# A transformer layer with an expert block: where and in what portions the dense gate table is written to DRAM

## The chip, the cores and the metric

The kernel runs on one core of one Trainium2 chip. The metric is the device time of one execution in microseconds (us), as a median over several runs. The engines named below are TensorE (PE, matmuls; PEld is its weight load), VectorE (DVE), ScalarE (ACT), GpSimd (POOL) and SyncE (SP). SP, ACT and POOL also issue DMAs; a "q" behind the name (ACTq) means the engine's own sequencer, which waits, branches and issues.

## The reference

256 latent tokens pass through one layer: a token mixer, and then a PEER block, which is what matters here. Each token has 8 heads, each head picks 16 of 16384 single-neuron experts, and the block sums the picked experts:

```
idx = e1 * PEER_NKEYS + e2
g = jax.nn.softmax(sc, axis=-1)
u_sel = jnp.take(u_tab, idx, axis=0)
act = jax.nn.gelu(jnp.einsum('td,thkd->thk', hb, u_sel))
v_sel = jnp.take(v_tab, idx, axis=0)
return jnp.einsum('thk,thkd->td', (g * act.astype(jnp.float32)).astype(hb.dtype), v_sel)
```

## The kernel before, in words

The kernel does not gather the experts of each token. It multiplies all 256 tokens by all 16384 rows of `u_tab`, 128 rows at a time, in 128 steps (`u_step`), and writes the GELU of each 128 x 256 result into a table in DRAM, `agd`: one row per expert, and in it, for each half of the tokens (`t`), 128 activations and 128 gates. The gates come from the routing and are dense too, with zeros for experts that a token did not pick. Afterwards a list of the experts in use is made, and only their rows of `v_tab` and of `agd` are gathered, in 92 tiles of 128 rows (`N_L`), and multiplied on TensorE (`v_tile`).

Each float32 operand is split into a high and a low part (ACT at L252, then DVE at L253), and each product is made of three matmuls (`mm3`, L281 to L283). The split of a tile has two halves, one at the start of a step (`ahead2`) and one at k == 7 of the matmul loop (`behind`), and it runs two tiles ahead of the matmuls. The raw u tiles (1 MB each) lie in four slots, `O_RAW`; SP loads a slot again (`done`, `emit_load`, L102) as soon as the split of the tile in it has ended.

The work that has nothing to do with the u products (routing, gates, list) is a Python generator, `beneath`, which `fill` draws on once per `u_step`, behind the step's matmuls, up to a budget. So its instructions are spread over the steps in program order. The generator `gates` makes the gates in batches of 8 tokens: DVE builds one-hot matrices, PE multiplies them (`products`, L1041 and L1044), and ACT copies the result out of PSUM into one of two buffers `GC` (`keep`, L1051). One buffer holds 64 tokens (`HT`, a half tile): 128 x 128 x 64 values, 4 MB. When it is complete, `keep` writes it to `agd` with four DMAs of 1 MB on ACT's queue (L1056). There are four half tiles, so this happens four times. Behind it in ACT's program stand the GELU of the step (L1176) and the store of its 128 KB (L1177), and then the split of the next tile (L252). `places` (its first matmul is L1087) and `make_list` come after the gates.

Behind the last u step the second product begins. Its v rows come with indirect DMAs on POOL (`gather(n)`, 1 MB), the rows of `agd` with others (`act_rows(n)`), both issued by the helper line L894. Gathers 0 to 3 are issued from `beneath`; the later ones come from `emit_load`, each when a slot has become free: 4 to 7 when the u tiles 124 to 127 are split, 8 and 9 when the v tiles 0 and 1 are. DVE makes a tile's weights from the gathered rows (`weights`, L1187; `weights_low`, L1201) with a copy on ACT (L1196) in between. Between `act_rows(1)` and `act_rows(2)` lies a branch, `tc.If(more > 0)` (L1255), for lists that are too long; with these inputs it isn't taken.

Of the kernel before, what the change touches and what calls it, by code (L numbers as in the profile page):

```python
# [29 lines left out]
N_L = N_A + N_1  # L30
# [11 lines left out]
N_RAW, N_HL = 4, 5  # L42
# [8 lines left out]
def layer_kernel(ctx: ExitStack, tc: tile.TileContext, I, out, dbg=None):  # L51
    nc = tc.nc
# [35 lines left out]
    order = []  # L88
    pos = [0]
    loaded = set()  # L90

    def emit_load(i):
        if i < len(order):
            loaded.add(i)
            key, parts = order[i]
            if parts is None:
                if key[1] + N_RAW < N_L:
                    gather(key[1] + N_RAW)
                return
            base = O_RAW + (i % N_RAW) * D  # L100
            for o, n, src in parts:
                nc.sync.dma_start(fa[:, base + o:base + o + n], src)  # L102
# [173 lines left out]
    def behind():  # L276
        if pending:
            pending.pop()()
# [583 lines left out]
    HT = 64  # L862
# [169 lines left out]

    def gates():
        def products(b):
            counts = pb[4 + b // NB][:, 0:P]
            oj, og = pair(b, P)
            for i in range(TB):
                oa = OHA[b % 2][:, i, :]  # L1040
                TE.matmul(counts, oa, oj[:, i, :], start=b % NB == 0 and i == 0,  # L1041
                          stop=b % NB == NB - 1 and i == TB - 1, skip_group_check=True)
                for q in range(2):
                    TE.matmul(pb[6 + i // 4][:, (i % 4) * P:(i % 4 + 1) * P], oa, og[:, i, q, :],  # L1044
                              start=i % 4 == 0 and q == 0, stop=q == 1, skip_group_check=True)

        def keep(b):
            c, o = divmod(b, HT // TB)
            for x in range(2):
                tl = slice(o * TB + 4 * x, o * TB + 4 * x + 4)  # L1050
                S.activation(GC[c % 2][:, :, tl], pb[6 + x].rearrange("p (t j) -> p j t", j=P), AF.Copy,  # L1051
                             scale=1.0 / GSC)
            if o == HT // TB - 1:
                for x in range(4):
                    cs = slice(32 * x, 32 * x + 32)
                    S.dma_start(ag4[cs, :, c // 2, 1, (c % 2) * HT:(c % 2 + 1) * HT].rearrange("c e i -> e c i"),  # L1056
                                GC[c % 2][:, cs, :])

        for b in range(2 * NB + 2):
            sl = slice(b * TB, (b + 1) * TB)  # L1060
            if b < 2 * NB:
                one_hot(OHA[b % 2], E2T[:, sl], P)
                one_hot(pair(b, P)[0], E1T[:, sl], P)
            yield 2300
            if b < 2 * NB:
                scaled(b, GT[:, sl, :], P)
            if b > 1:
                keep(b - 2)
            if 0 < b <= 2 * NB:
                products(b - 1)  # L1070
            yield 2400
# [75 lines left out]
    def beneath():  # L1147
        yield from routing()
        yield from list_tables()
        yield from gates()  # L1150
        yield from places()
        yield from make_list()
        for n in range(N_RAW):
            yield from (0 for _ in starts(NU - 16 + 3 * n))
            gather(n)
            yield 100
# [7 lines left out]
    def u_step(n, fill):  # L1164
# [3 lines left out]
        for k in range(KD):  # L1168
# [2 lines left out]
            mm3(bank, h[:, es], l[:, es], HH[:, k, :], HL[:, k, :], k == 0, k == KD - 1)  # L1171
            if k == 7:
                behind()
        fill()
        st = STAGE[n % 3]
        S.activation(st, bank, AF.Gelu_apprx_tanh)  # L1176
# [65 lines left out]
    at[0] = NU  # L1242
    for _ in work:
        pass

    for n in range(2):
        act_rows(n)


    V.tensor_reduce(flag[:, 0:1], flag, axis=AX.X, op=ALU.add)  # L1250
# [104 lines left out]

    for n in range(2, 4):
        act_rows(n)
    for n in range(2):
        weights(n)
        weights_high(n)  # L1360
        weights_low(n)
# [91 lines left out]
```

## Time and profile before

| | |
|---|---|
| median of 3 runs | 1862.34 us (1862.03 to 1863.49) |
| the profiled execution's own time | 1861.65 us |
| its span in the trace | 1859.7 us |
| TensorE busy | 1723.9 us, 93% of the span |
| VectorE, ScalarE, GpSimd busy | 70%, 47%, 14% |
| mean granted TensorE clock | 0.97 of full speed |
| u steps | from about 597 us to 1458 us |
| v tiles | from about 1468 us |

The span is the time from the first to the last instruction in the trace; the profiled execution took about 2 us more than it. The granted clock is the share of full speed that TensorE ran at; 1.00 is 2.4 GHz and 0.50 is 1.2 GHz.

### The profile page before, as it was taken

Reading aid. Unit: us, or ns where it says so; the run is one execution under the profiler, and the core shown is the slowest. Engines: PE = TensorE matmul, PEld = TensorE weight load, DVE = VectorE, ACT = ScalarE, POOL = GpSimd, SP = SyncE. Lnnn points to the kernel's source line nnn. Section 1 sums busy time; section 2 is a strip of 40 time slices with the busy share of each in tenths; the row PEclk is TensorE's granted clock in tenths of the full one; section 3 lists DMA queues with packets and bytes.
Section 4 is the critical chain, followed back from the end, with each engine's and each line's share of the span. In section 5 each row is a group of like instructions: output and inputs, shape, how many; then the busy total and the mean of one; then the engine's idle time right before and its main releaser. Section 6 shows DMA issues by size and latency. Waiting matters only on the chain.

```text
span 1859.7 us, 30150 instructions
## 1 busy us (share of the span) xinstructions
PE 1723.9 (93%) x12361; PEld 1539.2 (83%) x12361; DVE 1304.4 (70%) x1804; ACT 868.8 (47%) x1104; POOL 252.3 (14%) x221
## 2 busy tenths in 40 slices
PE   4999999999999999997969979699999799999995
PEld 0778567888899999997969979699999688888884
DVE  1347696887879999885848574588644477777776
ACT  5224666643544444443434343334344456656654
POOL 0000000000100000000000000000100366656662
PEclk9999999999999999998989989799999899999998
DMA  9886868888796766557575766655766589888882
GB/s 389 321 320 255 323 272 320 325 318 332 288 338 239 240 225 203 191 184 210 178 213 170 202 195 187 184 192 190 253 235 204 195 317 340 311 306 306 308 307 80
DMA packets 165512, 472.67 MB, mean 254 GB/s; under 512 B 75924, under 2 KB 108872, under 8 KB 115192
## 3 DMA queue, kind: packets, MB, share of 16 engines
q1 hardware_dynamic: 42624, 303.58, 45.4%
q0 software_dynamic: 21120, 128.68, 19.5%
q10 hardware_dynamic: 101624, 38.42, 8.0%
q8 instruction: 98, 1.61, 0.3%
q14 instruction: 46, 0.38, 0.1%
HBM read 432.81 MB, written 37.83 MB: 253 GB/s over the span
## 4 chain that ended last, share of the span: by engine, by line
PE 76%; DVE 8%; DMA 6%; ACTq 5%; ACT 3%; issue 2%; POOL 0%; SPq 0%; DVEq 0%; POOLq 0%
PE bank L281 23%; PE bank L283 23%; PE bank L282 23%; ACTq L1056 4%; DVE ra L253 2%; DMA fa<-in_wm_a_dram 2%; PE bank L1044 2%; ACT ra L252 1%; DMA fa<-in_wm_c_dram 1%; PE bank L361 1%; PE bank L306 1%; DVE fa L287 1%; PE bank L524 1%; ACTq L1177 1%; PE bank L1041 1%
## 5 line engine op out<-in xcount | busy, mean ns | idle before, releaser
L281 PE MATMUL bank<-ra 128*128 128x256 f32 (+1 forms) x3412 | 1059.5, 311 | 15.4 <-ACT ra L1196 14.3
L283 PE MATMUL bank<-ra 128*128 128x256 f32 (+1 forms) x3412 | 1048.6, 307 | 7.3 <-DVE ra L1201 4.6
L282 PE MATMUL bank<-ra 128*128 128x256 f32 (+1 forms) x3412 | 1047.4, 307 | 1.3 <-DVE ra L253 1.3
L253 DVE TENSOR_TENSOR ra<-fa,ra 128x1024 fp32r<-128x1024 f32 x564 | 683.1, 1222 | 398.9 <-ACT ra L252 393.5
L252 ACT ACTIVATE ra<-fa 128x1024 fp32r<-128x1024 f32 x564 | 592.4, 1058 | 520.2 <-PE bank L282 214.2
L281 PEld LDWEIGHTS bank<-ra 128*128 128x128 f32 x3412 | 656.1, 192 | 73.8 <-issue 25.5
L283 PEld LDWEIGHTS bank<-ra 128*128 128x128 f32 x3412 | 655.0, 192 | 40.0 <-DVE ra L1201 7.4
L282 PEld LDWEIGHTS bank<-ra 128*128 128x128 f32 x3412 | 656.0, 192 | 31.1 <-DVE ra L253 2.4
L1176 ACT ACTIVATE fa<-bank 128x256 f32<-128x256 f32 x128 | 49.1, 383 | 258.6 <-PE bank L283 191.9
L894 POOL DMA_INDIRECT fa<-in_peer_v_dram,fa x92 | 97.0, 1054 | 352.2 <-DVE ra L253 175.7
L894 POOL DMA_INDIRECT fa<-agd,fa x92 | 130.2, 1416 | 37.0 <-issue 26.5
L1021 DVE TENSOR_TENSOR fa<-fa 128x1024 f16<-128x1024 bf16 x96 | 108.1, 1168 | 0.0
L1030 DVE TENSOR_TENSOR fa<-fa 128x2048 f16<-128x2048 f16 (+1 forms) x48 | 100.2, 2088 | 0.8
L1044 PE MATMUL bank<-fa 128*128 128x128 f16 x512 | 49.8, 227 | 40.2 <-ACT fa L1051 24.9
L1044 PEld LDWEIGHTS <-fa 128*128 128x128 f16 x512 | 41.6, 102 | 40.6 <-issue 40.6
L1111 POOL DMA_DIRECT2D ptab<-fa x1 | 0.6, 581 | 546.5 <-DVE fa L1107 546.5
L287 DVE SCALAR_TENSOR_TENSOR fa<-fa 128x2048 f32<-128x2048 f32 x32 | 72.8, 2282 | 0.0
L361 PE MATMUL bank<-fa 128*2 128x512 f32 x256 | 40.7, 729 | 25.1 <-DMA fa<-in_wm_a_dram 16.8
L1196 ACT ACTIVATE ra<-fa 128x128 fp32r<-128x128 f32 x92 | 32.4, 352 | 48.7 <-DVE fa L1187 48.5
L1187 DVE TENSOR_TENSOR fa<-fa 128x128 f32<-128x128 f32 x92 | 33.6, 365 | 24.5 <-DMA fa<-agd,fa 24.1
L1041 PE MATMUL bank<-fa 128*128 128x128 f16 x256 | 47.9, 228 | 0.0
L306 PE MATMUL bank<-fa 128*2 128x512 f32 x256 | 34.1, 620 | 8.8 <-DMA fa<-in_wm_c_dram 8.8
(256 smaller groups left out, 960.2 us busy)
## 6 DMA issues: line engine op xcount, KB each, us to landing
fa<-in_peer_u_dram SPq DMA_DIRECT2D x128, 1024.0 KB, 5.1
fa<-in_wm_a_dram SPq DMA_DIRECT2D x32, 1024.0 KB, 7.7
fa<-in_wm_c_dram SPq DMA_DIRECT2D x32, 1024.0 KB, 7.1
fa<-in_wm_d_dram SPq DMA_DIRECT2D x32, 1024.0 KB, 6.5
fa<-in_w_in_dram SPq DMA_DIRECT2D x24, 1024.0 KB, 5.1
fa<-in_w_out_dram SPq DMA_DIRECT2D x16, 1024.0 KB, 7.1
fa<-in_wq_dram SPq DMA_DIRECT2D x16, 1024.0 KB, 7.1
agd<-fa ACTq DMA_DIRECT2D x128, 128.0 KB, 4.4
```

The costliest lines, as they stand in the source:

```text
L252: S.activation(h, x, AF.Copy)
L253: V.tensor_tensor(l, x, h.bitcast(F32), op=ALU.subtract)
L281: TE.matmul(dst, wh, mh, start=first, stop=False, skip_group_check=skip)
L282: TE.matmul(dst, wh, ml, start=False, stop=False, skip_group_check=skip)
L283: TE.matmul(dst, wl, mh, start=False, stop=last, skip_group_check=skip)
L287: V.scalar_tensor_tensor(junk, w, 1.0, s, op0=ALU.mult, op1=ALU.mult, accum_out=dst)
L894: G.indirect_dma_start(out=dst, out_offset=None, in_=src, in_offset=bass.IndirectOffsetOnAxis(ap=idx, axis=0), bounds_check=bound, oob_is_ ...
L1021: V.tensor_tensor(dst, iota_b[:, 0:n].unsqueeze(1).to_broadcast([P, TB, n]), numbers.unsqueeze(2).to_broadcast([P, TB, n]), op=ALU.is_equal)
L1030: V.tensor_tensor(og, oj.unsqueeze(2).to_broadcast([P, TB, 2, n]), factors.unsqueeze(3).to_broadcast([P, TB, 2, n]), op=ALU.mult)
L1041: TE.matmul(counts, oa, oj[:, i, :], start=b % NB == 0 and i == 0, stop=b % NB == NB - 1 and i == TB - 1, skip_group_check=True)
L1044: TE.matmul(pb[6 + i // 4][:, (i % 4) * P:(i % 4 + 1) * P], oa, og[:, i, q, :], start=i % 4 == 0 and q == 0, stop=q == 1, skip_group_check ...
L1056: S.dma_start(ag4[cs, :, c // 2, 1, (c % 2) * HT:(c % 2 + 1) * HT].rearrange("c e i -> e c i"), GC[c % 2][:, cs, :])
```

## The change

There are two parts. A finished half tile is no longer written at once: `keep` puts sixteen pieces of 256 KB (8 of the 128 columns each) on a list, and every `u_step` takes one of them off for SP's queue and every third step another one for ACT's, behind the step's matmuls and ahead of `fill`. Before a new half tile begins, whatever is left of the half tile before the last is written on ACT's queue. `beneath` waits for the list to be empty before gather 0. The second part: gathers 6 and 7 are no longer issued when their slots become free, but one behind `act_rows(0)` and `act_rows(1)`, ahead of the branch, and the other behind `act_rows(2)` and `act_rows(3)`.

```diff
+    late = []
...
             if parts is None:
-                if key[1] + N_RAW < N_L:
+                if key[1] in (2, 3):
+                    late.append(key[1] + N_RAW)
+                elif key[1] + N_RAW < N_L:
                     gather(key[1] + N_RAW)
                 return
...
+    pieces = []
+
+    def store_piece(eng):
+        if pieces:
+            c, x = pieces.pop(0)
+            cs = slice(8 * x, 8 * x + 8)
+            eng.dma_start(ag4[cs, :, c // 2, 1, (c % 2) * HT:(c % 2 + 1) * HT].rearrange("c e i -> e c i"),
+                          GC[c % 2][:, cs, :])
...
             c, o = divmod(b, HT // TB)
+            if o == 0:
+                while pieces and pieces[0][0] < c - 1:
+                    store_piece(S)
...
             if o == HT // TB - 1:
-                for x in range(4):
-                    cs = slice(32 * x, 32 * x + 32)
-                    S.dma_start(ag4[cs, :, c // 2, 1, (c % 2) * HT:(c % 2 + 1) * HT].rearrange("c e i -> e c i"),
-                                GC[c % 2][:, cs, :])
+                pieces.extend((c, x) for x in range(16))
...
         yield from make_list()
+        while pieces:
+            yield 0
...
             if k == 7:
                 behind()
+        store_piece(nc.sync)
+        if n % 3 == 0:
+            store_piece(S)
         fill()
...
     for n in range(2):
         act_rows(n)
+    gather(late.pop(0))
...
     for n in range(2, 4):
         act_rows(n)
+    gather(late.pop(0))
```

How the instructions stand now: first ACT, where the first half tile is complete, before the change. `fb` is the buffer `GC[0]`, `fa` holds among others `GC[1]`, and bank_80 and bank_81 are the PSUM banks of the gate products.

```order
L252 ACTIVATE ra<-fa 128x1024 x2
L1051 ACTIVATE fb<-bank_80 128x128x4
L1051 ACTIVATE fb<-bank_81 128x128x4
L1056 DMA agd<-fb 128x32x64 x4
L1176 ACTIVATE fa<-bank_76 128x256
L1177 DMA agd<-fa 256x1x128
L252 ACTIVATE ra<-fa 128x1024 x2
```

And ACT in the change a few steps later, around the first piece that goes by its queue (L1193 is the GELU, L1194 its store, L255 the split, L1066 the copy out of PSUM, L1044 the store of a piece).

```order
L1193 ACTIVATE fa<-bank_74 128x256
L1194 DMA agd<-fa 256x1x128
L255 ACTIVATE ra<-fa 128x1024 x2
L1044 DMA agd<-fb 128x8x64
L1066 ACTIVATE fa<-bank_80 128x128x4
L1066 ACTIVATE fa<-bank_81 128x128x4
L1193 ACTIVATE fa<-bank_75 128x256
L1194 DMA agd<-fa 256x1x128
L255 ACTIVATE ra<-fa 128x1024 x2
```

The four stores in a row have become single ones of a quarter of the size between the split and the GELU. Of a half tile's sixteen pieces four go this way; the other twelve stand on SP's queue, which in the change reads from the first half tile on as follows (before, it is 124 loads of u tiles in a row at this place).

```order
L105 DMA fa<-in_peer_u_dram 128x2048 x46
L1044 DMA agd<-fb 128x8x64
L105 DMA fa<-in_peer_u_dram 128x2048
L1044 DMA agd<-fb 128x8x64
L105 DMA fa<-in_peer_u_dram 128x2048
L1044 DMA agd<-fb 128x8x64
```

The loads and the pieces alternate, one of each a step, for 48 steps.

The third place is POOL around the branch, before the change, with what each instruction waits for. DMASW0 to DMASW7 count the landings of POOL's own DMAs, which take the eight of them in turn; DMAHW0 to DMAHW7 those of SP and ACT. The `ISA` row stands on the side of the branch that is taken here.

```order
L894 DMA fa<-in_peer_v_dram,fa 128x2048 [waits DMASW7_49,DVE_49]
L894 DMA fa<-in_peer_v_dram,fa 128x2048 [waits DMASW0_49,DVE_49]
L894 DMA fa<-agd,fa 128x256 [waits DMAHW4_49,DMAHW5_49,DMAHW3_49,DMAHW6_49,DMAHW2_49,DMAHW7_49,DMAHW1_49,DMASW1_49]
L894 DMA fa<-agd,fa 128x256 [waits DMASW2_49,PE_49]
L1254 TENSOR_LOAD fa [waits DVE_49]
L1255 COMPARE_AND_BRANCH
...
L1255 ISA [waits DMASW4_49,DMASW5_49,DMASW3_49,DMASW6_49,DMASW2_49,DMASW7_49,DMASW1_49,DMASW0_49]
...
L894 DMA fa<-agd,fa 128x256 [waits DMASW5_49,PE_49]
L894 DMA fa<-agd,fa 128x512 [waits DMASW6_49]
```

And the same place in the change.

```order
L897 DMA fa<-in_peer_v_dram,fa 128x2048 [waits DMASW6_49,DMASW0_49,DVE_49]
L897 DMA fa<-agd,fa 128x256 [waits DMAHW4_49,DMAHW5_49,DMAHW3_49,DMAHW6_49,DMAHW2_49,DMAHW7_49,DMAHW1_49,DMAHW0_49]
L897 DMA fa<-agd,fa 128x256 [waits PE_49]
L897 DMA fa<-in_peer_v_dram,fa 128x2048 [waits DMASW1_49]
L1273 TENSOR_LOAD fa [waits DVE_49]
L1274 COMPARE_AND_BRANCH
...
L1274 ISA [waits DMASW4_49,DMASW5_49,DMASW3_49,DMASW6_49,DMASW2_49,DMASW7_49,DMASW1_49,DMASW0_49]
...
L897 DMA fa<-agd,fa 128x256 [waits DMASW4_49,PE_49]
L897 DMA fa<-agd,fa 128x512 [waits DMASW5_49]
L897 DMA fa<-in_peer_v_dram,fa 128x2048 [waits DMAHW0_49,DMASW6_49]
```

Gather 6 now stands between the first two row fetches and the branch, and gather 7 behind the next two; on the far side of the branch POOL waits for all eight counters, as it did before.

## Rows read from the trace of the kernel before

**Rows 1.** The page's part 1: busy time, share of the span, instructions.

```profile
PE 1723.9 (93%) x12361; PEld 1539.2 (83%) x12361; DVE 1304.4 (70%) x1804; ACT 868.8 (47%) x1104; POOL 252.3 (14%) x221
```

**Rows 2.** The page's part 4: the chain that ended last, by engine.

```profile
PE 76%; DVE 8%; DMA 6%; ACTq 5%; ACT 3%; issue 2%; POOL 0%; SPq 0%; DVEq 0%; POOLq 0%
```

**Rows 3.** Timeline of ACT, first complete half tile: start, length, instruction, idle before.

```profile
853.79 16.74 ACTq L1056 DMA_DIRECT2D agd<-fb  x4
870.58 0.38 ACT L1176 ACTIVATE fa<-bank 128x256 f32<-128x256 f32 x1 [16.82 <-issue]
870.99 3.73 ACTq L1177 DMA_DIRECT2D agd<-fa  x1
```

**Rows 4.** Waits of PE, 840 to 1200 us: total, times, longest us.

```profile
PE bank L1044 <- ACT fa L1051: 24.9, 2, 12.5
PE bank L1087 <- DVE fa L1083: 20.3, 1, 20.3
PE bank L1044 <- ACT fb L1051: 15.3, 1, 15.3
```

**Rows 5.** Windows: an undisturbed stretch, then 10 us behind each idle stretch.

```profile
884.00:954.00 70.00, 70.00 (x660) 69.74 (x659) 56.28 (x43) 32.70 (x45) 0.00 (x0) 1.00 0.55 183
880.18:890.18 10.00, 10.00 (x92) 9.96 (x92) 8.80 (x8) 4.17 (x7) 0.00 (x0) 0.81 0.65 224
977.65:987.65 10.00, 10.00 (x76) 10.00 (x76) 8.82 (x7) 3.13 (x5) 0.00 (x0) 0.74 0.39 120
1078.68:1088.68 10.00, 10.00 (x96) 9.96 (x96) 9.04 (x8) 4.36 (x8) 0.00 (x0) 0.84 0.65 224
1179.41:1189.41 10.00, 10.00 (x68) 10.00 (x69) 7.15 (x22) 1.94 (x3) 0.00 (x0) 0.75 0.41 128
```

**Rows 6.** DMA queues while the first half tile is stored, 853 to 877 us.

```profile
q10 hardware_dynamic: 16720, 4.33, 84.8%
```

**Rows 7.** Store line L1056: from issue to landing.

```profile
DMA to landing us min/median/max: 8.8/10.9/13.0
```

**Rows 8.** Load line L102, 850 to 1250 us: issues, and landings.

```profile
L102 SPq DMA_DIRECT2D fa<-in_peer_u_dram x51: 327/328/328, 854.1 to 1248.2; - x51
...
DMA to landing us min/median/max: 4.8/5.0/6.6
```

**Rows 9.** Store line L1177, 880 to 954 us: issues.

```profile
L1177 ACTq DMA_DIRECT2D agd<-fa x11: 520/521/521, 880.9 to 949.8; - x11
```

**Rows 10.** Timeline of ACT in an undisturbed step with gates.

```profile
899.11 1.06 ACT L252 ACTIVATE ra<-fa 128x1024 fp32r<-128x1024 f32 x1 [0.66 <-PE bank L282]
...
902.11 0.38 ACT L1176 ACTIVATE fa<-bank 128x256 f32<-128x256 f32 x1 [0.97 <-PE bank L283]
```

**Rows 11.** Timeline of POOL from the last early gather to the third row fetch.

```profile
1457.38 0.99 POOL L894 DMA_INDIRECT fa<-in_peer_v_dram,fa  x1 [4.77 <-DVE fa L1252]
1464.65 1.00 POOL L894 DMA_INDIRECT fa<-agd,fa  x1 [6.28 <-DMA agd<-fa]
1465.96 1.00 POOL L894 DMA_INDIRECT fa<-agd,fa  x1 [0.30 <-issue]
1470.56 1.00 POOL L894 DMA_INDIRECT fa<-agd,fa  x1 [3.60 <-DMA fa<-in_peer_v_dram,fa]
```

**Rows 12.** Line L1255, the branch: POOL's own instructions.

```profile
L1255 POOLq EVENT_SEMAPHORE  x4: 17/42/43, 1468.6 to 1468.9; - x4
...
L1255 POOLq INC_SWDGE_SEM  x1: 731/731/731, 1469.0 to 1469.0; - x1
```

**Rows 13.** Line L894, 1428 to 1470 us: from issue to landing.

```profile
DMA to landing us min/median/max: 2.8/5.8/6.1
```

**Rows 14.** The chain from 1464 to 1477 us: start, length, what.

```profile
1470.56 2.72 DMA fa<-agd,fa
```

**Rows 15.** Timeline of PE where the third v tile begins.

```profile
1476.41 0.50 PE L283 MATMUL bank<-ra 128*128 128x512 f32 x1 [0.67 <-DVE ra L1201]
```

**Rows 16.** Windows: 10 us behind two short idle stretches, 480 us.

```profile
483.22:493.22 10.00, 10.00 (x66) 10.00 (x67) 8.20 (x15) 7.79 (x11) 0.25 (x1) 0.76 0.98 368
```

More of the change, by code (lines that the diff above doesn't have):

```diff
@@ L1244, in layer_kernel @@
         pass
+    assert not pieces
     for n in range(2):
         act_rows(n)
+    gather(late.pop(0))
     V.tensor_reduce(flag[:, 0:1], flag, axis=AX.X, op=ALU.add)
```

## The prediction

> **What bounds the kernel now.** I read the page first. TensorE is busy for 93% of the span [rows 1], and the chain of work that ended last runs through it for 76% [rows 2]. So only idle time of TensorE, or time at its lower clock, can be won. One share in that chain is odd: ACTq, the sequencer of ScalarE, has 5%. A sequencer computes nothing; it issues.
>
> The timeline of ACT shows what it is. When a half tile of gates is complete, the four stores of 1 MB hold ACT's sequencer for 16.74 us; the GELU comes only then, and the store of its rows takes another 3.73 us to issue [rows 3] where 0.52 us is usual [rows 9]. The split of the next tile stands behind all this. ACT is out for some 21 us. TensorE lives on tiles that are already split, and then it runs dry.
>
> The waits of PE show how long: three idle stretches before line L1044 (two that sum to 24.9 us, one of 15.3) and one of 20.3 before L1087, the first matmul of `places` [rows 4]. These are the four half tiles. Together 24.9 + 15.3 + 20.3 = **60.5 us**.
>
> Each is followed by a time at the lower clock. In the 10 us behind them the mean granted clock is 0.81, 0.74, 0.84 and 0.75, and 1.00 in the undisturbed stretch between [rows 5]. PE has work all through these windows, so they lose (0.19 + 0.26 + 0.16 + 0.25) x 10 = **8.6 us**. In the undisturbed stretch TensorE is busy 70.00 of 70.00 us, DVE 56.28 and ACT 32.70 [rows 5]: PE alone is the bound there.
>
> **Part 1, the stores in pieces.** *What they cost the DMA engines.* While the first half tile is stored, ACT's DMA queue fills 84.8% of 24 us with 16720 packets [rows 6]: 0.848 x 24 x 16 / 16720 is 19.5 ns of one engine for a packet, nearly all of them 256 bytes. A half tile has 128 x 128 = 16384 packets, whatever DMAs they belong to. A piece has 1024, over 16 engines 64 each: 1.25 us. Row stores in the undisturbed stretch are issued from 880.9 to 949.8 us, eleven of them [rows 9]: 6.9 us a step. The engines are 0.55 busy there [rows 5], 3.8 us a step. One piece on SP and a third of one on ACT add 1.33 x 1.25 = 1.7 us: 5.5 of 6.9 us. It fits, at a share of about 0.8.
>
> *What they cost SP.* An issue of a u load takes 0.33 us [rows 8], and SP has nothing else to do. A load lands in 5.0 us [rows 8]. It refills the slot of a tile just split, and that slot is read again four splits on, three steps and more: 3 x 6.9 = 20.7 us, so it lands some 15 us early. A piece ahead of it delays it by 1.25 us, a second on ACT's queue by as much again. Hidden.
>
> *What they cost ACT.* Sixteen issues. What holds ACT in the burst is that an issue waits while the packets of the one before are still being fed. A piece is issued alone, behind the second split of a step; until the row store two things stand between, the copies and the GELU, and ACT even idles for 0.97 us before that GELU [rows 10]. From the end of the split (900.17) to the end of the GELU (902.49) are 2.3 us; a piece needs 1.25 us of the engines plus a start. If the row store still waits as long as behind the burst, 3.73 us, that falls on every third step, and ACT idles for (70 - 32.70) / 70 x 6.9 = 3.7 us of each step [rows 5]. Hidden, and the lead of the split tiles covers a single delay: about 21 us of hold gave only 12.5 us of idle PE.
>
> *The buffers.* A list of sixteen is emptied in 12 steps (12 on SP, 4 on ACT), a half tile takes 13 or more, and the copy that overwrites a buffer stands two steps (13.8 us) behind the last piece. The big stores took 8.8 to 13.0 us to land [rows 7], of which a quarter of the packets is the smaller part. No wait, though by the slowest of these values it would be near.
>
> *What is left.* `places` still needs a few DVE operations before its first matmul; without the stall behind it I leave 0 to 2 us, say 0.8, below what shortens the clock. Part 1: 60.5 + 8.6 - 0.8 = **68.3 us** won, bounds 58 and 69.
>
> The Trainium skill speaks against it: "DMA: Bandwidth & Descriptors", Rules for kernel authors, asks for DMAs of at least 1 MiB for full bandwidth, and the anatomy section of the same page fits 2.0 us plus the bytes at 436 GB/s to a DMA. By that fit 64 pieces instead of 16 stores cost 48 x 2.0 = 96 us more, an estimate, and if they lay on the path the change would end at about 1862 - 68 + 96 = 1890 us. The rows say that it is the packets that cost (19.5 ns each, however cut) and that an issue doesn't wait for the landing: the four issues took 16.74 us in all where each store took 8.8 us or more to land [rows 3, 7].
>
> **Part 2, the gathers.** Before, POOL issues gather 9 at 1457.38, the row fetches at 1464.65 and 1465.96, and the third fetch at 1470.56 [rows 11]. The first fetch waits for the last row store, not for gathers 6 and 7, which were issued 12 and more us earlier; nothing there becomes earlier, since gathers 8 and 9 stay where they were, right ahead of that store. What matters is the branch. POOL's own instructions at L1255 are four semaphore waits from 1468.6 to 1468.9 and one that raises the counters, 0.73 us [rows 12]; by the order they cover all eight counters of POOL's DMAs. The page gives the wait to a v gather, but gather 9 was in by 1457.38 + 6.1 = 1463.5; the second row fetch, with 2.8 us to landing [rows 13], was in at 1468.8. So POOL passes the branch when the **last DMA in flight** has landed, and in the change that is gather 6: issued 1.3 us behind the second fetch, at 1467.3, and 5.8 to 6.1 us in flight [rows 13], in at 1473.2. That is 1473.2 - 1468.8 = **4.4 us later**, and with it the third row fetch, at 1475.0.
>
> Who waits for that: it lands 2.72 us after its issue [rows 14], DVE makes the weights of the third v tile, and PE starts that tile at 1476.41 after an idle time of 0.67 us already [rows 15]. The cover is 0, so all 4.4 us are idle time, 5.1 with what was there. Behind an idle stretch the clock falls: the losses above are 1.6 to 2.6 us for stretches of 12 to 20 us, and 2.4 us (0.76) where two short stretches at 480 us preceded [rows 16]. I take 2.0 (bounds 0 and 3). Gather 7 then runs ahead of the fifth row fetch, and each of the later gathers is about 5 us later, as PE is; 0 to 2 us, I take 0. Part 2: 4.4 + 2.0 = **6.4 us** lost, bounds 0 and 10.
>
> **Sum.** Span 1859.7 - 68.3 + 6.4 = 1797.8. The median shown is 2.6 us above the span of the profiled execution, which itself took 2 us more than its span: 1797.8 + 2.6 = **1800.4 us**, 3.3% less.
>
> **The rivals.**
> - *The branch costs nothing*: gather 6 is in before POOL gets through (the fetch of code behind the branch would have to take as long), or PE finds other work. The rows show no reserve at the third tile. Then part 2 is 0 to 1: about 1794 us. Chance 0.14.
> - *Pieces still stall ACT*: row stores behind ACT's sixteen pieces wait longer than ACT idles, or a copy of a new half tile waits for the last piece, twice, 5 us each plus 2 of clock; or the stall of `places` stays for a few us. For it: landings up to 13.0 us [rows 7]. Against it: PE's lead. About 1807 to 1818 us. Chance 0.17.
> - *Slower than before*: SP's queue works through load and piece one after the other, each to its landing. A big store lands 8.8 us after its issue at the least [rows 7], 3.8 more than the 5.0 us of the engines (4096 packets); a piece would be 1.25 + 3.8 = 5.0 us, a load 5.0, together 10 of a 6.9 us step, 3.1 us lost in 48 steps, 149 us: about 1950 us. It decides from 62 / 48 = 1.3 us a step on, that is from pieces of 3.2 us. Against it: ACT's queue holds several stores in flight [rows 3, 7]. Chance 0.03. The skill's 2.0 us per DMA is the same mechanism with a smaller price, and the trace disagrees in the same way.
> - *The drain is worse*: gather 7 and the later row fetches keep PE short for several tiles, DMA being full in the v tiles; another 6 us, about 1806. Chance 0.06.
>
> **The numbers.** The forecast has 0.60. I predict its time, 1800.4. The range 1791 to 1811 holds it, the free branch, the worse drain and the smaller stalls of the second rival. A measurement tells 0.2% (3.7 us) from no change. Faster holds in every case but the third and a part of what I haven't seen: 0.95; same 0.02; slower 0.03.
>
> **What would show it.** No entry of ACTq in the chain of note; no idle PE over 3 us and a clock of 1.00 from 850 us to the end of the u steps; u loads landing in 5 to 8 us; DMA share near 0.8 there. At the branch POOL's semaphore waits end about 7 us behind the second row fetch instead of 2.9, and PE has an idle stretch of about 5 us before the third v tile. It is wrong if the half tiles still show idle stretches, if loads land later than 15 us, or if PE passes the third v tile without a gap.

## The result, and the profile after

The changed kernel takes **1798.9 us** (median of 4 runs, 1797.2 to 1800.47) against 1862.18 us of the kernel before in the same comparison (4 runs, 1859.59 to 1863.49): a ratio of 0.9662, with a 95% interval of 0.9645 to 0.9678. The forecast was 1800.4 us in a range of 1791 to 1811. The profiled execution took 1797.54 us, with a span of 1795.7 us.

In the changed kernel the lines have moved: the split is L255 and L256, the three matmuls are L284 to L286, the pieces are issued at L1044, the GELU and the store of its rows are L1193 and L1194, the copy and the low part of a v tile's weights L1213 and L1218, the gathers L897, the branch L1274.

The page's part 1 and part 4 of the changed kernel, to be read against [rows 1, 2]:

```profile
PE 1716.5 (96%) x12361; PEld 1532.8 (85%) x12361; DVE 1305.2 (73%) x1804; ACT 871.1 (49%) x1104; POOL 254.6 (14%) x221
...
PE 84%; DVE 8%; DMA 5%; ACT 2%; issue 1%; SPq 0%; POOLq 0%; DVEq 0%; POOL 0%; ACTq 0%
```

TensorE does the same 12361 matmuls in 7 us less busy time, since fewer of them run at the lower clock, and ScalarE's sequencer has gone from the chain.

The stretch with all four half tiles, in the changed kernel: the window from 840 to 1200 us (length, then busy us of PE, PEld, DVE, ACT and POOL, granted clock, DMA share, GB/s), and the waits of PE in it:

```profile
840.00:1200.00 360.00, 359.67 (x3332) 358.00 (x3332) 284.83 (x251) 164.28 (x219) 0.58 (x1) 1.00 0.81 229
...
PE bank L1099 <- DVE fa L1095: 0.3, 1, 0.3
```

Of the four idle stretches of [rows 4] one of 0.3 us is left, the one at the first matmul of `places`, and the clock is 1.00 throughout. What ACT and SP do for it stands in the rows of the store, load and row store lines of the changed kernel:

```profile
L1044 SPq DMA_DIRECT2D agd<-fb x24: 385/426/1619, 860.1 to 1099.5; - x24
L1044 SPq DMA_DIRECT2D agd<-fa x24: 385/427/1664, 946.1 to 1178.6; - x24
...
L1044 ACTq DMA_DIRECT2D agd<-fb x8: 362/366/404, 870.3 to 1089.6; - x8
L1044 ACTq DMA_DIRECT2D agd<-fa x8: 364/366/367, 950.5 to 1163.7; - x8
...
DMA to landing us min/median/max: 2.6/6.5/10.0
...
DMA to landing us min/median/max: 5.0/5.5/7.3
...
L1194 ACTq DMA_DIRECT2D agd<-fa x56: 520/521/540, 840.7 to 1198.5; - x56
```

The first landing row is that of the pieces, the second that of the u loads. A piece takes 0.4 us of a sequencer in the median, up to 1.66 us on SP and never more than 0.40 us on ACT, and the row store issues in its usual 0.52 us every time, where it took 3.73 us behind the burst [rows 3].

At the branch, the changed kernel's POOL has one long entry. The first fence is the timeline of POOL, the second its own instructions at the branch; [rows 11, 12] are the same places before:

```profile
1387.37 0.99 POOL L897 DMA_INDIRECT fa<-in_peer_v_dram,fa  x1 [4.77 <-DVE fa L1271]
1394.76 1.00 POOL L897 DMA_INDIRECT fa<-agd,fa  x1 [6.40 <-DMA agd<-fa]
1396.07 1.00 POOL L897 DMA_INDIRECT fa<-agd,fa  x1 [0.30 <-issue]
1397.37 1.00 POOL L897 DMA_INDIRECT fa<-in_peer_v_dram,fa  x1 [0.30 <-issue]
1404.93 1.00 POOL L897 DMA_INDIRECT fa<-agd,fa  x1 [6.57 <-PE bank L286]
```

```profile
L1274 POOLq EVENT_SEMAPHORE  x4: 17/43/4245, 1398.8 to 1399.1; - x4
...
L1274 POOLq COMPARE_BRANCH  x1: 58/58/58, 1396.2 to 1396.2; - x1
L1274 POOLq INC_SWDGE_SEM  x1: 707/707/707, 1403.4 to 1403.4; - x1
```

Gather 6 is issued at 1397.37 us behind the second fetch, and one semaphore wait, of 17 to 43 ns elsewhere, now takes 4.245 us. The page puts the 6.57 us before the third fetch down to a matmul; the semaphore rows are the ones to trust, for the fetch leaves 0.87 us behind the end of POOL's last branch instruction in both kernels (1404.06 to 1404.93 here, 1469.69 to 1470.56 before). And the wait ends where gather 6 lands: the landing is at 1403.28 us in the trace, the end of the wait at 1403.31. The third fetch leaves 8.86 us behind the second (1404.93 - 1396.07), where it was 4.60 us before [rows 11].

TensorE at the first v tiles, in the changed kernel and then in the kernel before, from the timeline (idle time in brackets) and the windows:

```profile
1398.23 0.79 PE L284 MATMUL bank<-ra 128*128 128x512 f32 x1 [10.48 <-ACT ra L1213]
1408.35 0.60 PE L284 MATMUL bank<-ra 128*128 128x512 f32 x1 [2.76 <-ACT ra L1213]
1409.14 0.80 PE L285 MATMUL bank<-ra 128*128 128x512 f32 x1 [0.20 <-DVE ra L256]
1410.76 0.80 PE L286 MATMUL bank<-ra 128*128 128x512 f32 x1 [0.82 <-DVE ra L1218]
...
1398.23:1408.23 10.00, 7.36 (x24) 5.62 (x24) 1.42 (x5) 1.50 (x4) 2.82 (x4) 0.82 0.39 126
1408.35:1418.35 10.00, 8.98 (x26) 6.57 (x27) 9.05 (x13) 6.82 (x10) 6.46 (x7) 0.66 0.95 347
```

```profile
1468.22 0.80 PE L281 MATMUL bank<-ra 128*128 128x512 f32 x1 [10.46 <-ACT ra L1196]
...
1479.80 0.50 PE L283 MATMUL bank<-ra 128*128 128x512 f32 x1 [0.34 <-DVE ra L1201]
...
1468.22:1478.22 10.00, 9.33 (x34) 7.26 (x35) 5.22 (x10) 4.90 (x8) 4.49 (x5) 0.86 0.18 54
1478.22:1488.22 10.00, 9.66 (x43) 7.67 (x42) 8.85 (x12) 6.55 (x9) 6.46 (x7) 1.00 0.97 367
```

The 10.5 us ahead of the first v tile are as before. Ahead of the third tile there is a new idle stretch of 2.76 us, and behind it the clock falls to 0.66.

**A ruler for the runs below.** The medians of like kernels differ by up to 3 us, so the profiled execution is cut in two at the GELUs: from the first GELU to the last (the u steps, where part 1 acts), and from the last GELU to the end of the span (the tail, where part 2 acts). The rows of the GELU line, of the kernel before and of the changed one:

```profile
L1176 ACT ACTIVATE fa<-bank x128: 361/384/388, 596.6 to 1457.8; 128x256 f32<-128x256 f32 x128
```

```profile
L1193 ACT ACTIVATE fa<-bank x128: 361/386/387, 594.8 to 1387.8; 128x256 f32<-128x256 f32 x128
```

Before, the u steps take 1457.8 - 596.6 = 861.2 us and the tail 1859.7 - 1457.8 = 401.9; after, 793.0 and 1795.7 - 1387.8 = 407.9. The change wins **68.2 us** in the u steps and loses **6.0 us** in the tail. The rest of the 64.0 us between the two spans, 1.8 us, stands ahead of the u steps, which the change doesn't touch.

The tail of one execution is still a coarse measure: its last part takes 70 to 73 us, and differs by 2.8 us between two kernels whose v tiles are alike (e1 and e4 below). A finer mark lies ahead of them, the start of ACT's copy for the 81st of the 92 v tiles, counted from the start of the last GELU. These are the copies of before, of the changed kernel, of e3, e11 and e12, from the timelines of ACT:

```profile
1788.87 0.30 ACT L1196 ACTIVATE ra<-fa 128x128 fp32r<-128x128 f32 x1
1723.90 0.30 ACT L1213 ACTIVATE ra<-fa 128x128 fp32r<-128x128 f32 x1
1723.48 0.30 ACT L1213 ACTIVATE ra<-fa 128x128 fp32r<-128x128 f32 x1
1718.22 0.30 ACT L1199 ACTIVATE ra<-fa 128x128 fp32r<-128x128 f32 x1
1718.40 0.30 ACT L1196 ACTIVATE ra<-fa 128x128 fp32r<-128x128 f32 x1
```

Before, it starts 1788.87 - 1457.8 = 331.1 us behind the last GELU, in the changed kernel 336.1.

### The profile page after: what moved, and what is told of

Same layout as the page of the kernel before. It is cut to its first block, busy times and chain, and to the rows that moved or that the text cites. A ratio compares the mean times of both kernels' runs of the same rounds, so it can differ in the third digit from the quotient of the medians.

```text
span 1795.7 us, 30223 instructions
## 1 busy us (share of the span) xinstructions
PE 1716.5 (96%) x12361; PEld 1532.8 (85%) x12361; DVE 1305.2 (73%) x1804; ACT 871.1 (49%) x1104; POOL 254.6 (14%) x221
## 4 chain that ended last, share of the span: by engine, by line
PE 84%; DVE 8%; DMA 5%; ACT 2%; issue 1%; SPq 0%; POOLq 0%; DVEq 0%; POOL 0%; ACTq 0%
PE bank L284 26%; PE bank L286 25%; PE bank L285 25%; DMA fa<-in_wm_a_dram 2%; DVE ra L256 2%; PE bank L1056 2%; DMA fa<-in_wm_c_dram 1%; PE bank L364 1%; PE bank L527 1%; PE bank L309 1%; DVE fa L290 1%; PE bank L1053 1%; ACT ra L255 1%; DVE fa L941 1%; DMA fa<-agd,fa 1%
## 5 line engine op out<-in xcount | busy, mean ns | idle before, releaser
L284 PE MATMUL bank<-ra 128*128 128x256 f32 (+1 forms) x3412 | 1057.7, 310 | 17.1 <-ACT ra L1213 16.0
L286 PE MATMUL bank<-ra 128*128 128x256 f32 (+1 forms) x3412 | 1047.4, 307 | 7.0 <-DVE ra L1218 4.3
L256 DVE TENSOR_TENSOR ra<-fa,ra 128x1024 fp32r<-128x1024 f32 x564 | 683.9, 1223 | 332.8 <-ACT ra L255 326.8
L255 ACT ACTIVATE ra<-fa 128x1024 fp32r<-128x1024 f32 x564 | 593.6, 1058 | 509.7 <-PE bank L285 216.2
L284 PEld LDWEIGHTS bank<-ra 128*128 128x128 f32 x3412 | 653.8, 192 | 75.7 <-issue 24.6
L286 PEld LDWEIGHTS bank<-ra 128*128 128x128 f32 x3412 | 653.6, 192 | 39.3 <-DVE ra L1218 6.2
L1193 ACT ACTIVATE fa<-bank 128x256 f32<-128x256 f32 x128 | 49.2, 384 | 204.5 <-PE bank L286 196.7
L897 POOL DMA_INDIRECT fa<-in_peer_v_dram,fa x92 | 97.3, 1058 | 351.8 <-DVE ra L256 174.7
L897 POOL DMA_INDIRECT fa<-agd,fa x92 | 132.3, 1438 | 40.1 <-issue 26.5
L1213 ACT ACTIVATE ra<-fa 128x128 fp32r<-128x128 f32 x92 | 32.4, 352 | 48.0 <-DVE fa L1204 47.9
L1056 PE MATMUL bank<-fa 128*128 128x128 f16 x512 | 46.3, 219 | 0.0
L1053 PE MATMUL bank<-fa 128*128 128x128 f16 x256 | 44.8, 220 | 0.0
L345 ACT ACTIVATE fa<-bank,fa 128x256 f32<-128x256 f32 x32 | 16.3, 561 | 52.1 <-PE bank L342 35.2
```

Of the source, the lines that this page charges most:

```text
L255: S.activation(h, x, AF.Copy)
L256: V.tensor_tensor(l, x, h.bitcast(F32), op=ALU.subtract)
L284: TE.matmul(dst, wh, mh, start=first, stop=False, skip_group_check=skip)
L286: TE.matmul(dst, wl, mh, start=False, stop=last, skip_group_check=skip)
L897: G.indirect_dma_start(out=dst, out_offset=None, in_=src, in_offset=bass.IndirectOffsetOnAxis(ap=idx, axis=0), bounds_check=bound, oob_is_ ...
```

## The experiments

The theory for part 1 is that of the prediction: what was lost is time of ACT's sequencer, which an issue holds while the packets of the one before it are fed. Its rival is that the burst itself is too much, of full DMA engines or of large DMAs, wherever it is issued. For part 2 the theory is that POOL passes the branch only when the last DMA in flight has landed; its rival is that moving the gathers costs by itself, since they run late, and not where they stand.

| kernel | median us | ratio to before, 95% interval | u steps us | 81st copy us | tail us |
|---|---|---|---|---|---|
| before (profiled execution) | 1862.18 | 1 | 861.2 | 331.1 | 401.9 |
| changed | 1798.9 | 0.9662 (0.9645 to 0.9678) | 793.0 | 336.1 | 407.9 |
| e1_pieces_only | 1794.93 | 0.9635 (0.9619 to 0.9650) | 792.9 | 330.8 | 404.0 |
| e2_gathers_only | 1867.91 | 1.0032 (1.0022 to 1.0042) | 861.9 | 336.3 | 406.4 |
| e3_behind_branch | 1795.79 | 0.9643 (0.9629 to 0.9658) | 792.8 | 333.0 | 403.2 |
| e4_stores_on_sp | 1793.78 | 0.9635 (0.9618 to 0.9651) | 792.8 | 330.7 | 401.1 |
| e5_all_on_act | 1792.89 | 0.9631 (0.9614 to 0.9648) | 792.8 | 330.7 | 401.1 |
| e6_half_pieces | 1793.24 | 0.9634 (0.9616 to 0.9651) | 792.9 | 330.6 | 400.5 |
| e7_gather9_late | 1790.15 | 0.9622 (0.9604 to 0.9640) | 792.9 | 327.8 | 398.3 |
| e9_two_ahead | 1802.6 | 0.9679 (0.9666 to 0.9692) | 792.9 | 339.4 | 410.8 |
| e10_four_ahead | 1790.82 | 0.9612 (0.9597 to 0.9628) | 792.7 | 327.7 | 398.1 |
| e11_gather9_again | 1789.91 | 0.9611 (0.9596 to 0.9626) | 792.9 | 327.7 | 400.6 |
| e12_sp_again | 1790.98 | 0.9619 (0.9604 to 0.9634) | 792.7 | 330.7 | 401.3 |
| c1_changed_again | 1799.44 | 0.9666 (0.9644 to 0.9688) | 792.9 | 336.7 | 408.0 |

The runs e1 to e4 stood beside one another on one chip, so did e5, e6, e7 and e9, and so did the last four of the table; the median of before was 1861.33, 1861.70 and 1862.53 us there. Medians are compared closely only within such a group.

**e1_pieces_only: part 1 alone.** Against the changed kernel the gathers go back to where they were:

```diff
-                if key[1] in (2, 3):
-                    late.append(key[1] + N_RAW)
-                elif key[1] + N_RAW < N_L:
+                if key[1] + N_RAW < N_L:
...
-    gather(late.pop(0))
```

> The changed kernel without its second part: gates in pieces, all gathers issued where they were before. Theory (gather 6 in flight holds POOL at the branch, 4.2 us in the changed kernel's trace, and the idle stretch lowers TensorE's clock): about 6.4 us less than the changed kernel's 1798.9, so 1792.5 us (1791 to 1794), POOL's waits at the branch back to under 0.3 us, idle time of PE between the first and the fourth v tile back to 1.0 us. Rival (the two gathers cost nothing, the difference lies elsewhere in the v tiles): 1798 to 1800 us.

1794.93 us, 0.9 us above the range expected, and u steps of 792.9 us: all of part 1's gain is there. POOL's longest wait at the branch is 219 ns, and the new gap ahead of the third v tile is gone. Timeline of PE in this kernel:

```profile
1401.88 0.79 PE L282 MATMUL bank<-ra 128*128 128x512 f32 x1 [10.61 <-ACT ra L1211]
1410.20 0.50 PE L284 MATMUL bank<-ra 128*128 128x512 f32 x1 [0.82 <-DVE ra L1216]
```

**e2_gathers_only: part 2 alone.** The kernel before, with the moved gathers and the stores as they were:

```diff
-                if key[1] + N_RAW < N_L:
+                if key[1] in (2, 3):
+                    late.append(key[1] + N_RAW)
+                elif key[1] + N_RAW < N_L:
...
     for n in range(2):
         act_rows(n)
+    gather(late.pop(0))
...
     for n in range(2, 4):
         act_rows(n)
+    gather(late.pop(0))
```

> The kernel before with the second part alone: four stores of 1 MB on ScalarE's queue as before, gathers 6 and 7 behind the row fetches. Theory: slower than before by the same 6.4 us, 1862.2 + 6.4 = 1868.6 us, with a wait of some 4.2 us at the branch. Rival (the gathers only cost where the pieces have changed the load on the DMA engines): no difference, 1862 us. The hope behind the move (row fetches land sooner since fewer gathers are ahead of them): up to 2 us faster, 1860 us.

1867.91 us, 6.6 us slower than before beside it (0.22% to 0.42%), with the four idle stretches of the half tiles in place (24.9, 20.4 and 15.2 us). The branch and PE, as in the changed kernel:

```profile
L1259 POOLq EVENT_SEMAPHORE  x4: 17/43/3622, 1472.2 to 1472.4; - x4
...
1481.26 0.80 PE L284 MATMUL bank<-ra 128*128 128x512 f32 x1 [2.94 <-ACT ra L1199]
```

So part 2 is a loss by itself: 5.2 us at the 81st copy, 5.0 in the changed kernel. In the medians the two parts add up roughly: -66.4 and +6.6 against the -63.3 of the whole change, measured on different chips.

**e3_behind_branch: both gathers late, both behind the branch.** They run behind the fourth row fetch:

```diff
     for n in range(2):
         act_rows(n)
-    gather(late.pop(0))
...
     for n in range(2, 4):
         act_rows(n)
     gather(late.pop(0))
+    gather(late.pop(0))
```

> The changed kernel with gather 6 issued behind the branch: both late gathers follow the fourth row fetch. Theory (it is the landing of what is in flight at the branch that counts, not that the gathers come late): nearly all of the 6.4 us comes back, 1792.5 to 1795 us. Rival (two late gathers put 2 MB ahead of the fifth and sixth row fetch, and PE starves there wherever they are issued): 1798 us or more.

Both gathers run late here too, gather 6 8.5 us behind the first row fetch in place of 2.6, gather 7 9.8 in place of 12.8. Most of the loss is gone: 1795.79 us, 0.9 us more than e1 beside it, where the two intervals overlap, though 0.8 us above the range expected. The waits at the branch, in this kernel:

```profile
L1273 POOLq EVENT_SEMAPHORE  x4: 17/43/43, 1401.8 to 1402.1; - x4
L1273 POOLq COMPARE_BRANCH  x1: 58/58/58, 1398.7 to 1398.7; - x1
```

So lateness isn't the main cost: of the 5.0 us at the 81st copy 1.9 are left. But this rest is there: no kernel with the gathers as before stands later than 331.1 us at this mark, e3 stands at 333.0. The fifth row fetch now runs behind both gathers and lands 7.2 us after its issue, 2.9 before; and the clock of the first 10 us of v tiles was 0.71, 0.86 before. Which of the two made the 1.9 us, no run tells.

**e9_two_ahead: both gathers ahead of the branch.** The opposite dose:

```diff
     for n in range(2):
         act_rows(n)
     gather(late.pop(0))
+    gather(late.pop(0))
...
     for n in range(2, 4):
         act_rows(n)
-    gather(late.pop(0))
```

> The changed kernel with gather 7 ahead of the branch too, right behind gather 6: the suspected cost doubled. Theory (POOL passes the branch when the last DMA in flight has landed): 1 MB more behind gather 6 takes 3.5 to 4.1 us, so a wait of about 8 us at the branch in place of 4.2, the third row fetch as much later, and about 1798.9 + 4 = 1803 us, 10 us over the pieces alone. Rival (one late gather costs a fixed wait): 1799 us, no change.

```profile
L1275 POOLq EVENT_SEMAPHORE  x4: 17/43/6545, 1402.2 to 1409.0; - x4
...
1414.10 0.80 PE L284 MATMUL bank<-ra 128*128 128x512 f32 x1 [6.34 <-ACT ra L1213]
```

With no, one and two gathers in flight at the branch the longest wait is 0.04, 4.2 and 6.5 us, the gap at the third v tile none, 2.76 and 6.34 us, the tail 403.2, 407.9 and 410.8 us. The second gather was issued 1.3 us behind the first and prolonged the wait by 2.3 us. I had expected a wait of about 8 us; the order is as the theory says, the size is smaller. The landing came as reckoned, 3.4 us behind that of gather 6 (1408.89 against 1405.45), but POOL reached its long wait 0.9 us later behind gather 6 than in the changed kernel. So the third row fetch is the better measure: it leaves 4.62, 8.86 and 12.16 us behind the second with none, one and two gathers. And the wait ends with the last landing wherever there is one to wait for: 1403.28 and 1403.31 us in the changed kernel, 1404.73 and 1404.76 in c1, 1476.04 and 1476.07 in e2, 1408.89 and 1408.92 here.

**e4_stores_on_sp: no pieces, one word.** The kernel before with its four stores of 1 MB on SP's queue:

```diff
-                    S.dma_start(ag4[cs, :, c // 2, 1, (c % 2) * HT:(c % 2 + 1) * HT].rearrange("c e i -> e c i"),
+                    nc.sync.dma_start(ag4[cs, :, c // 2, 1, (c % 2) * HT:(c % 2 + 1) * HT].rearrange("c e i -> e c i"),
```

> The kernel before with one word changed: the four 1 MB stores of a half tile are issued from SP's queue instead of ScalarE's, not in pieces; gathers as before. Theory A (what is lost is ScalarE's sequencer, held while an issue waits): SP is held for some 17 us instead, its u loads come 17 us late where they land about 15 us early, so 0 to 6 us idle of PE for each half tile, 1793 to 1820 us. Rival B (the loss comes from the DMA engines being full for 20 us, so that loads and row stores starve, and only small pieces help): most of the four idle stretches stay, 1845 to 1862 us.

1793.78 us, u steps of 792.8 us: the whole gain of the pieces, with the same burst of 1 MB stores. Timelines of SP and ACT in this kernel, first half tile:

```profile
855.67 0.33 SPq L102 DMA_DIRECT2D fa<-in_peer_u_dram  x1
856.10 17.76 SPq L1056 DMA_DIRECT2D agd<-fb  x4
873.95 4.54 SPq L102 DMA_DIRECT2D fa<-in_peer_u_dram  x1
...
856.32 0.38 ACT L1176 ACTIVATE fa<-bank 128x256 f32<-128x256 f32 x1 [0.97 <-PE bank L283]
856.74 0.52 ACTq L1177 DMA_DIRECT2D agd<-fa  x1
857.65 1.06 ACT L252 ACTIVATE ra<-fa 128x1024 fp32r<-128x1024 f32 x1 [0.94 <-ACT fa L1176]
```

SP is held for 17.76 us, as ACT was for 16.74 [rows 3], and its next load for another 4.54 us. But TensorE doesn't notice: loads land in 13.1 us at the most; ACT waits for such a load five times from 840 to 1200 us, 10.7 us in all, and the lead of the split tiles covers that (PE waits for 0.3 us in the same window). ACT issues its row store in 0.52 us *in the middle of the burst*, on other queues of the same DMA engines. The rival of part 1 falls: neither full DMA engines nor large DMAs cost anything here, only the hold of ACT's sequencer. The Trainium skill, "DMA: Bandwidth & Descriptors", section "Issuing engines are not separate DMA queues", says that issuing from several engines saves only the sequencer's issue time, usually small beside the DMA. The rows agree with the first half; the issue time wasn't small here, 16.74 us for stores that landed in 8.8 to 13.0 us [rows 3, 7], and it was the whole loss.

**e5_all_on_act: pieces, but none on SP.**

```diff
-        store_piece(nc.sync)
+        store_piece(S)
         if n % 3 == 0:
             store_piece(S)
```

> The pieces of 256 KB, but all of them on ScalarE's queue at the same rate (one a step, two on every third step), gathers as before. Theory (ScalarE is idle for 3.7 us of a 6.9 us step, so a hold by a single piece of 1 to 4 us hides, and SP isn't needed): within 3 us of the pieces on both queues, 1795 to 1798 us. Rival (ScalarE can't carry them): part of the four stalls is back, 1805 us or more.

**e6_half_pieces: 128 KB instead of 256 KB.** Thirty-two pieces per half tile, two at a time:

```diff
-            cs = slice(8 * x, 8 * x + 8)
+            cs = slice(4 * x, 4 * x + 4)
...
-        store_piece(nc.sync)
+        for _ in range(2):
+            store_piece(nc.sync)
         if n % 3 == 0:
-            store_piece(S)
+            for _ in range(2):
+                store_piece(S)
```

> Pieces of half the size: 32 of 128 KB for a half tile, two a step on SP and two on every third step on ScalarE, gathers as before. Theory (the packets cost, 19.5 ns each however they are cut, and landings are waited for by nobody): the time of the pieces of 256 KB, 1794 to 1796 us. Rival (each DMA has a fixed cost that the queues pay one after the other, 2 us by the Trainium skill's DMA page, section on the anatomy of one DMA): 64 DMAs more would take up to 128 us more of the queues, and where SP or ScalarE can't hide it, over 1800 us. The first sentences hold without that page.

Both have the gathers as in e1, and both are at the time of e1 or a little under it, on another chip and somewhat under what I had expected: 1792.89 and 1793.24 us, u steps of 792.8 and 792.9 us. The issues of the pieces in e5, then one row of e6:

```profile
L1042 ACTq DMA_DIRECT2D agd<-fb x32: 362/366/1101, 858.9 to 1098.3; - x32
L1042 ACTq DMA_DIRECT2D agd<-fa x32: 364/366/2425, 944.9 to 1177.4; - x32
```

```profile
L1042 SPq DMA_DIRECT2D agd<-fb x48: 359/498/1524, 859.9 to 1099.8; - x48
```

The second of two pieces in a row on ACT's queue holds it for 2.4 us once, and for 1.1 us at the most elsewhere, which is less than the 3.7 us that it idles in a step. So the engine that issues doesn't matter either with holds as short as these; where between 2.4 and 16.74 us a hold begins to cost, no run shows. Sixty-four more DMAs than in e1 change nothing that can be measured. By the fit of 2.0 us per DMA that the Trainium skill gives ("DMA: Bandwidth & Descriptors", the anatomy of a DMA, where it is measured on DMAs that GpSimd issues; these are SP's and ACT's), they would cost 64 x 2.0 = 128 us, an estimate, if they lay on the path; no run here shows any of it.

**e7_gather9_late: one gather less ahead of the last row store.** From e4, with gather 9 alone moved behind the fourth row fetch:

```diff
-                if key[1] + N_RAW < N_L:
+                if key[1] == 5:
+                    late.append(key[1] + N_RAW)
+                elif key[1] + N_RAW < N_L:
...
     for n in range(2, 4):
         act_rows(n)
+    gather(late.pop(0))
```

> Stores of 1 MB on SP's queue, and of the gathers only number 9 is issued late, behind the fourth row fetch and the branch; 6 and 7 where they were before. Theory: the first row fetch waits for the last row store, and this store's packets come behind the 1 MB of gather 9, issued 0.8 us ahead of it (it lands 5.7 us after its issue, where 4.3 is usual and 2.7 the least); without it the fetch comes 1.4 to 3 us earlier, and the idle stretch of 10.6 us ahead of the v tiles is that much shorter: 1790.5 to 1792.5 us against 1793.8. Rival (the store's own way to DRAM sets its landing): no change, 1793.8 us.

**e11_gather9_again and e12_sp_again** are e7 and e4 once more, **c1_changed_again** is the changed kernel once more, beside one another; **e10_four_ahead** is e7 with four row fetches ahead of the branch:

```diff
-    for n in range(2):
+    for n in range(4):
         act_rows(n)
...
-    for n in range(2, 4):
-        act_rows(n)
     gather(late.pop(0))
```

> The version with 1 MB stores on SP and gather 9 late once more, beside the others of this call on one chip. Theory: 2.4 to 3 us less than with the gathers as before, since the idle stretch ahead of the v tiles is 2.8 us shorter, and 6 to 9 us less than the changed kernel. Rival: the difference of the first run was scatter between chips, less than 1 us here.

> Stores of 1 MB on SP, gathers as before, once more beside the others. Theory: 5 to 6.5 us less than the changed kernel beside it, and 2.4 to 3 us more than with gather 9 late. Rival: the same time as with gather 9 late.

> As the version with 1 MB stores on SP and gather 9 late, but all four first row fetches stand ahead of the branch. Theory (with gather 9 late PE has no idle time left at the third v tile, so the branch hides already): no change against it, within 1.5 us. Rival (the branch still costs PE a wait that doesn't show as one): 2 us or more less.

> The changed kernel itself on the same chip as the three other runs of this call, so that differences of a few us can be read within one chip: 1797 to 1801 us by its own earlier times. Theory: 5 to 6.5 us over the stores on SP. Rival (the second part costs nothing): the same time.

With gather 9 out of its way the last row store lands sooner, 2.9 to 3.0 us after its issue (e7, e10, e11) in place of 5.7 to 5.9 (before, the changed kernel, e4, e12), and the idle stretch ahead of the first v tile is shorter. Timeline of PE in e12, then in e11:

```profile
1398.28 0.80 PE L281 MATMUL bank<-ra 128*128 128x512 f32 x1 [10.57 <-ACT ra L1196]
```

```profile
1398.28 0.79 PE L284 MATMUL bank<-ra 128*128 128x512 f32 x1 [7.81 <-ACT ra L1199]
```

The idle stretch is 2.8 us shorter, but the medians differ by only 1.1 us (1789.91 against 1790.98), where I had expected 2.4 to 3; the intervals of the two ratios overlap. The 81st copy settles what the medians don't: it starts at 327.7 to 327.8 us in the three profiles with the late gather 9 (e7, e10, e11), and at 330.6 to 331.1 in the six with the same branch and gathers as before (before, e1, e4, e5, e6, e12). So the v tiles run some 3 us earlier; how much of it is left at the end, the scatter of the last 70 us hides. The tails are 398.3, 398.1 and 400.6 us against 401.9, 404.0, 401.1, 401.1, 400.5 and 401.3, 2.7 us less in the mean.

e10 shows that four fetches ahead of the branch are worth nothing more, as expected. It shows one thing besides: its fourth fetch is still in flight at the branch, and the longest wait there is 2.56 us, but the mark is the same 327.7 us. That wait costs nothing, since the four fetches that TensorE needs first stand ahead of it.

The three runs beside c1 all beat the changed kernel: e11 by 9.5 us, 0.9611 (0.9596 to 0.9626) against 0.9666 (0.9644 to 0.9688). Both e11 and e12 beat it by more than I had expected: e12 by 8.5 us, where I had said 5 to 6.5. At the 81st copy e12 is 6.0 us ahead of c1; the rest lies in the last 70 us and ahead of the u steps.

## Why the prediction was right

**Part 1, right in mechanism and size.** The sum was 60.5 us of idle time, 8.6 of low clock, less 0.8 that would stay: 68.3. The u steps became 68.2 us shorter. The idle time that stayed is 0.3 us; this term was set too high by 0.5, and with 0.3 in its place the sum is 0.6 above what was measured. What I predicted of the rows came as said: a share of the DMA engines of 0.81 (0.8), loads that land in 5.0 to 7.3 us (5 to 8), a clock of 1.00, no ACTq in the chain. One bound was needlessly wide: that ACT's row store might wait 3.73 us behind a piece. It never waited, 0.54 us at the most.

That the *cut* was needed was never claimed by the sum, but it was implied by costing the pieces at length, and e4 shows that it was not: SP's queue does it with stores of 1 MB. (Such stores on POOL's queue, or spaced out on ACT's, were not tried.) The rivals "pieces still stall ACT" and "slower than before" are out by the rows of the changed kernel; the latter needed a queue that works its DMAs one by one, and in the changed kernel a load (5.5 us to landing) and a piece (6.5 us, both in the median) went out in each of 48 steps of some 6.5 us (56 row stores from 840.7 to 1198.5 us), and the u steps were no longer for it. The 2.0 us per DMA of the Trainium skill, which I set against part 1, are fitted to DMAs that GpSimd issues ("DMA: Bandwidth & Descriptors", the anatomy of a DMA). Here SP and ACT issue them, and nothing of it lay on the path.

**Part 2, right in mechanism, and the sum right for partly wrong terms.** The wait was predicted from the flight of gather 6, 5.8 to 6.1 us; it landed at 1403.28, 5.9 us behind its issue, and the third row fetch left 4.3 us later behind the second (4.4 predicted). That my base fitted is in part luck: I took POOL to be held until the second fetch landed (1468.8), but its waits there took 0.04 us [rows 12], and POOL came to them only at 1468.6, 3.0 us behind its compare of the branch. e3, e2, the changed kernel and e9 show that the wait is the main cause: without a gather in flight it is 0.04 us, and all but 1.9 us of the loss is gone with it. The rival "the branch costs nothing" is out, and so is "the drain is worse": from the 31st copy to the 81st the changed kernel stays the same 5.0 us behind the kernel before.

The terms below it were mis-sized in opposite directions. *"The cover is 0, so all 4.4 us are idle time"* failed: the idle time at the third tile grew by (2.76 + 0.20 + 0.82) - (0.67 + 0.34) = 2.8 us. The row on which I rested it [rows 15] is not the start of the tile but its *third* matmul, which needs the low part of the weights; the first two need only the high part. In the changed kernel they begin 2.4 us ahead of the third (1408.35 against 1410.76), so part of the delay was covered by work of the same tile. *"I take 2.0"* for the clock was too low: the two windows lose (0.18 + 0.34) x 10 = 5.2 us after and 0.14 x 10 = 1.4 before; but 0.20 + 0.82 = 1.0 us of the second window PE was idle at half speed, which counts as idle time already, so 0.5 goes off again, and 3.3 us more are lost. Together 2.8 + 3.3 = 6.1 by this account, 6.0 by the tail, 5.0 at the 81st copy, 6.4 predicted. That the gathers behind cost nothing more (I took 0) fits this. So the total of part 2 came out by two errors that cancel, 1.6 us too much idle time and 1.3 too little clock.

**The sum.** 1859.7 - 68.2 + 6.0 = 1797.5 would be the span against 1797.8 predicted; the 1795.7 seen has the 1.8 us ahead of the u steps in it, a stretch that varies between executions of every kernel (the first GELU begins at 594.7 to 599.0 us in the fourteen profiles).

## What to carry to other kernels

Stores of many small packets, issued one right behind the other, hold the sequencer of the engine that issues them: look in the timeline for DMA issues of several microseconds on an engine that also computes, and before cutting the stores, give them to a queue whose delay is covered by a lead; one word did here what sixteen pieces did. Where POOL passes a branch, put DMAs of several microseconds behind it and not ahead, since the last one in flight sets when it gets through; what is needed soon may stand ahead of it, as the fetches of e10 do. And cost an idle stretch with its shadow: here 2.8 us of idle time cost 3.3 us of clock behind it.

## What the runs showed of the hardware that I had not expected

- The hold of an issue belongs to one queue. In e4 the burst's stores take 4.6 to 4.7 us each in the median on SP, 8.2 at the longest, and an issue on ACT's queue beside them 0.52 to 0.58 us as ever, though both feed the same DMA engines. The first issue behind a pause takes 0.38 to 0.39 us even for 1 MB.
- POOL needs 2.6 to 3.1 us from the compare of the branch to its first wait, whatever is in flight (e3: 1398.7 to 1401.8; the changed kernel: 1396.2 to 1398.8). So a DMA that lands within that time costs no wait: before the change the second row fetch, with 2.8 us to landing [rows 13], landed in it, and the longest wait was 0.04 us.
- The window behind the short stretch of 2.76 us has a granted clock of 0.66, lower than those behind the stretches of 12 to 20 us in [rows 5]. It is 0.67 in e2 (2.94 us), 0.66 in c1 (2.59 us) and 0.67 in e9 (6.34 us), each behind some 7 us of matmuls that follow a first idle stretch of 10.4 to 10.6 us. So the clock cost about the same behind 2.6 and behind 6.3 us; why no less than behind the long ones, no run here tells.
